# The down product of a SwiGLU layer in four parts, two of them by seven products of halves, with the results added up in DRAM

## The chip, the cores and the metric

The kernel runs on one core of one Trainium2 chip. The metric is device time in microseconds from launch to end, the median of several runs. Everything is float32; each matrix product is made of three TensorE products of rounded parts (below), so that it keeps nearly float32 accuracy.

## The reference, cut to what matters

One encoder layer on 512 tokens of width 2048. Everything up to the last line is left alone by the change; the last line is what the change is about.

```python
h2 = rms_norm(x, ffn_norm_g)                      # 512 x 2048
act = jax.nn.silu(h2 @ w_ffn_gate) * (h2 @ w_ffn_up)   # 512 x 5632
return x + act @ w_ffn_down                       # w_ffn_down: 5632 x 2048
```

## The kernel before, in words

All tensors lie transposed: 128 features in the partitions, 512 tokens along the free dimension. So `act` is 44 tiles of 128x512 (`act0` to `act43`), the output is 16 tiles of 128x512 (column tiles `m`), and a weight block is 128x128. Eight blocks make one weight tile of 128x1024, which SP loads with one DMA (`wr`).

**A plain product.** Each operand is split into a rounded part and a residual: ACT casts (`wh`, `act` first half), DVE subtracts (`wl`, `act` second half). One block times one act tile is then three matmuls of 512 columns:

```python
def mm3(ps, ah, al, bh, bl, first, last, **kw):
    mm(ps, ah, bh, first, False, **kw)
    mm(ps, ah, bl, False, False, **kw)
    mm(ps, al, bh, False, last, **kw)
```

`group()` does this for one column tile over all act tiles that are in SBUF. The split weight tiles have three buffers each, so the cast of weight tile i waits until PE has done with tile i-3.

**By seven products of halves.** The function `seven()` returns `run()`, which the gates and the FFN's gate and up products use. It takes 16 row tiles of the weights as 8 pairs, the tokens in two halves of 256, and makes two column tiles (a "group") with seven products where eight would be the plain number (the Strassen-Winograd scheme). For that, each pair of input tiles must first become seven sums of 128x256: `x_sums()` (ACT: four copies `L793` to `L797`; DVE: four sums or differences `L795` to `L800`, the last three each made from the one before) writes them to `V`, and `x_split()` splits them into `X` (ACT `L809`: one cast of 128x1792; DVE `L810`: one residual of 128x1792). Of the weights, four sums are formed on DVE (`wsum`, `L835`), and seven operands are split on ACT and DVE (`wsplit`, `L841`, `L842`). One product is

```python
for p in range(p0, p1):
    x = xs[p][:, i * 2 * H:(i + 1) * 2 * H]
    mm(bank, hi[:, p * P:(p + 1) * P], x, first and p == 0, False, skip_group_check=True)
for p in range(p0, p1):
    x = xs[p][:, i * 2 * H:(i * 2 + 1) * H]
    mm(bank[:, H:], lo[:, p * P:(p + 1) * P], x, False, p == NP - 1, skip_group_check=True)
```

that is 8 matmuls of 512 and 8 of 256 columns; all eight pairs must be there before the first product of a group can be finished. A group is 112 matmuls.

**The down product before.** `act` goes to DRAM (`actd`, by DMAs that POOL issues), but for the first four tiles. The 44 act tiles are taken in three chunks, `DOWN = (12, 16, 16)`: ACT issues the loads of a chunk (`actr`), they are split, and each of the 16 column tiles is a `group()` over the chunk, 16 x 44 x 3 = 2112 matmuls of 512 columns. The sums over chunks are kept in SBUF (`dacc`, 16 tiles); with the last chunk the residual `x2d` is loaded from DRAM, added, and SP stores `out`. Loads and short-lived tiles share five buffers, `tmp`.

**What sets the order.** Each engine runs its instructions in the order that the scheduler wrote at build time, and an instruction that waits holds up everything behind it on its engine; ACT and POOL issue their DMAs from the same queue. Matmuls keep the order of the code.

Of the kernel before, what the change touches and what calls it, by code (L numbers as in the profile page):

```python
# [41 lines left out]
DOWN = (12, 16, 16)  # L42
# [15 lines left out]
def weight_blocks():  # L58
# [20 lines left out]
    def quarters(name, c0, c1):  # L79
        for half, c in ((0, c0), (0, c1), (1, c1), (1, c0)):  # L80
            out.extend((name, k * P, c, P) for k in range(half, KT, 2))
# [10 lines left out]
    f0 = 0  # L92
    for n in DOWN:
        first = WIDE if f0 == 0 else 0
        for k in range(n if first else 0):
            out += [("w_ffn_down", (f0 + k) * P, m * P, P) for m in range(first)]
        for m in range(first, KT):
            out += cols("w_ffn_down", m * P, n, k0=f0)
        f0 += n
# [3 lines left out]
def layer_kernel(tc, wpk, xT, par, flt, zemb, w4, decT, tbl, tb2, rope, qkg, out):  # L103
# [674 lines left out]
    def seven(nm, gi):  # L778

        gain = ("ffng", "mixg")[gi]  # L780
        late, xs, raws = {}, [None] * NP, {"n": 0}
# [4 lines left out]
        def x_sums(p, xe, xo):  # L786

            V = vp.tile([P, SQ], F32, tag="V", bufs=3, name=f"{nm}V{p}")
            b12 = ev(f"b12{p}")
            v = [V[:, i * H:(i + 1) * H] for i in range(7)]  # L790
            ge, go = pcol(gain, 2 * p), pcol(gain, 2 * p + 1)
            ngo = ngain[:, gi * KT + 2 * p + 1:gi * KT + 2 * p + 2]
# [32 lines left out]
        def group_raws(n):  # L825

            t = {}
            for q, name in ((0, "a11"), (3, "a12"), (1, "a21"), (2, "a22")) if n == 0 else \
# [31 lines left out]
        def run(groups, rows, c_tiles, finish, sums=None, side_pool=None, norm=None, tail=None):  # L860
# [4 lines left out]
            banks["pool"].release()  # L865
            psf = tc.alloc_tile_pool(name="psf" + nm, bufs=1, space=PSUM, reuse_waits="tile")
            banks.update(pool=psf, n=3)

            def bank(b, n):
                return psf.tile([P, S], F32, tag=b, bufs=2 if b == "x" else 1, name=f"{nm}{b}{n}")  # L870
# [3 lines left out]

            for n in range(groups):
                w0 = group_raws(n)
# [3 lines left out]
                if n == 0:  # L880
# [51 lines left out]
                if n > 0:  # L932
                    product(z, wsplit(w0["a12"], f"a12_{n}"), 1, True)
# [3 lines left out]
                if norm and n == 0:  # L937
# [7 lines left out]
                finish(n, (c0, c1))  # L945
            state.update(tile=raws["base"] + 4 * groups, pos=BLK)
            for name in ("cp", "rc", "xb"):
                late[name].release()
            return late["sg"]
# [50 lines left out]
    def gate_finish(n, c):  # L1000
        m = n + GATES_AHEAD
        for i, t in enumerate(c):
            nc.scalar.activation(t, t, AF.Sigmoid, bias=pcol("bgate", i * KT + m))
            b = tmp(f"br{i}{m}")
            nc.scalar.dma_start(b, bd[i][m])
            nc.vector.tensor_tensor(t, t, b, ALU.mult)
        nc.vector.tensor_tensor(c[0], c[0], c[1], ALU.add)
        nc.gpsimd.dma_start(md[m], c[0])
# [24 lines left out]
    sgp = run(KT - GATES_AHEAD, [r1], c_gates, gate_finish, tail=m_first())  # L1033
# [47 lines left out]
    def act_tile(j, pool, bufs):  # L1081
        t = pool.tile([P, 2 * S], F32R, tag="act", bufs=bufs, name=f"act{j}")
        acts[j] = (t[:, :S], t[:, S:])
        return acts[j]

    def act_split(j, src, pool, bufs):
        hi, lo = act_tile(j, pool, bufs)
# [11 lines left out]
    def swiglu(n, c):  # L1099
        j, up = n // 2 * 2, n % 2  # L1100
        if not up:
            for t in c:
                nc.vector.tensor_tensor(t, t, rbc2, ALU.mult)
                nc.scalar.activation(t, t, AF.Silu)
            gated[j] = c
            return
        for i, (t, g) in enumerate(zip(c, gated.pop(j))):
            nc.vector.tensor_tensor(t, t, g, ALU.mult)
            if j + i < EARLY_ACTS:
                act_split(j + i, t, ea, EARLY_ACTS)  # L1110
            else:
                nc.gpsimd.dma_start(actd[j + i], t)

    ea = None
    sgp = run(FT, [r1, sgp], c_ffn, swiglu, sums=lambda: x_sums(NP - 1, xt[-2], xt[-1]), side_pool=early_pool,
        norm=lambda: sumsq_add(acc2, xt[-1], KT - 1, "x2sq"))
    sgp.release()
    banks["pool"].release()


    psd = tc.alloc_tile_pool(name="psd", bufs=1, space=PSUM, reuse_waits="tile")
    banks.update(pool=psd, n=8)
    r3 = tc.alloc_tile_pool(name="r3d", bufs=1, reuse_waits="tile")
    r1 = tc.alloc_tile_pool(name="r1d", bufs=1, reuse_waits="tile")
    NA = DOWN[0] - EARLY_ACTS

    def act_load(j, pool, bufs):
        t = tmp(f"actr{j}")
        nc.scalar.dma_start(t, actd[j])
        act_split(j, t, pool, bufs)  # L1130

    dacc = [None] * KT

    def down(ci, f0, n, m, dp, done=False):
        last = ci == len(DOWN) - 1
        if ci == 0:
            dacc[m] = r3.tile([P, S], F32, tag="r", bufs=16, name=f"dacc{m}")
        if last:
            x2t = tmp(f"x2r{m}")
            nc.scalar.dma_start(x2t, x2d[m])  # L1140
            nc.vector.tensor_tensor(dacc[m], dacc[m], rbc2, ALU.mult)
            nc.vector.tensor_tensor(dacc[m], dacc[m], x2t, ALU.add)
        if not done:
            group(dp, [acts[j] for j in range(f0, f0 + n)])
        if ci == 0:
            nc.scalar.copy(dacc[m], dp)
        elif not last:
            nc.vector.tensor_tensor(dacc[m], dacc[m], dp, ALU.add)
        else:
            t = tmp(f"dt{m}")  # L1150
            nc.vector.tensor_tensor(t, dp, rbc2, ALU.mult)
            nc.vector.tensor_tensor(dacc[m], dacc[m], t, ALU.add)
            nc.sync.dma_start(out[m], dacc[m])

    f0 = 0
    for ci, n in enumerate(DOWN):
        if ci == 0:
            for j in range(EARLY_ACTS, n):
                act_load(j, r1, NA)
            dps = [ps_tile(f"d0{m}") for m in range(WIDE)]  # L1160
            for k in range(n):
                for dp in dps:
                    wh, wl = wblk()
                    mm3(dp, wh, wl, acts[k][0], acts[k][1], k == 0, k == n - 1)
            for m in range(WIDE):
                down(ci, f0, n, m, dps[m], True)
        elif ci == 1:
            for p in (ea, xa, wq):
                p.release()
            r1e = tc.alloc_tile_pool(name="r1e", bufs=1, side="right", reuse_waits="tile")  # L1170
            for j in range(f0, f0 + n):
                act_load(j, r1e, 24)
        else:
            for j in range(f0, f0 + n):
# [119 lines left out]
```

## Time and profile before

| what | us |
|---|---|
| runs before: median (lowest to highest of 3) | 2619.01 (2617.99 to 2620.55) |
| the profiled execution: its own time | 2624.83 |
| the profiled execution: span from the first to the last instruction | 2623.0 |
| mean granted TensorE clock in it | 0.993 |

In the profile PE is TensorE's matmuls, PEld its weight loads, DVE VectorE, ACT ScalarE, POOL GpSimd, SP SyncE; a "q" behind a name is that engine's DMA queue. Times in rows are us from the start of the span, unless ns is said. The rows are in the section before the prediction.

### The profile page before, as it was taken

How to read it: one execution, taken by the hardware profiler on the slowest of the kernel's cores; microseconds unless marked ns; L12 is line 12 of the kernel's file. 1: busy time of each engine (PE TensorE's matmuls, PEld its weight loads, DVE VectorE, ACT ScalarE, POOL GpSimd, SP SyncE). 2: the span in 40 equal slices, each digit the busy share in tenths (PEclk: the TensorE clock that was granted, in tenths of full speed). 3: DMA queues.
4: the chain of work that ended last, by engine and by line, in shares of the span. 5: the costliest groups of instructions: out<-in, count | busy, mean ns of one | idle time of the engine just before them, and what ended most of it. 6: DMA issues, size and time to landing. Idle time of an engine off the chain costs nothing.

```text
span 2623.0 us, 33908 instructions
## 1 busy us (share of the span) xinstructions
PE 2587.8 (99%) x13170; PEld 2200.4 (84%) x13170; DVE 1811.1 (69%) x2596; ACT 1117.1 (43%) x1652; POOL 115.2 (4%) x214
## 2 busy tenths in 40 slices
PE   9999999999999999999999999999999999999999
PEld 7788888878887888788788888888888888788887
DVE  7877763756556999654799898898898862443343
ACT  6444433657344445443454444444444442421111
POOL 1000011110000000000000000000000000000000
PEclk9999999999999999999999999999999999999999
DMA  6323233222454444544233333333333342432342
GB/s 221 109 94 115 93 115 107 81 68 100 170 185 146 145 144 156 169 161 145 93 113 121 113 129 121 113 129 126 112 125 129 114 148 96 165 132 97 129 146 106
DMA packets 107469, 333.08 MB, mean 127 GB/s; under 512 B 13067, under 2 KB 14603, under 8 KB 107308
## 3 DMA queue, kind: packets, MB, share of 16 engines
q1 hardware_dynamic: 72288, 251.69, 27.7%
q10 hardware_dynamic: 22284, 40.42, 5.0%
q0 software_dynamic: 12736, 38.81, 4.2%
q8 instruction: 103, 1.69, 0.3%
q14 instruction: 58, 0.48, 0.1%
HBM read 295.21 MB, written 35.65 MB: 126 GB/s over the span
## 4 chain that ended last, share of the span: by engine, by line
PE 80%; issue 14%; DVE 2%; ACT 1%; DMA 1%; POOL 1%; SPq 0%; ACTq 0%; POOLq 0%; DVEq 0%
PE fx L121 19%; PE d L121 18%; PE fy L121 9%; PE px L121 7%; PE o L121 6%; PE fz L121 5%; PE q L121 3%; PE phv L121 3%; PE b L121 3%; PE kv L121 2%; PE g L121 1%; PE up L121 1%; PE ab L121 1%; PE kp L121 1%; PE sp L121 1%
## 5 line engine op out<-in xcount | busy, mean ns | idle before, releaser
L173 DVE TENSOR_TENSOR wl<-wr,wh 128x1024 fp32r<-128x1024 f32 (+1 forms) x242 | 289.9, 1198 | 355.8 <-ACT wh L172 354.7
L172 ACT CAST wh<-wr 128x1024 fp32r<-128x1024 f32 (+1 forms) x242 | 249.8, 1032 | 638.7 <-PE d L121 302.5
L121 PE MATMUL d<-act,wh 128*128 128x512 f32 x1408 | 436.5, 391 | 1.6 <-DVE act L1089 0.9
L121 PEld LDWEIGHTS d<-act,wh 128*128 128x128 f32 x1408 | 264.9, 188 | 59.9 <-DVE act L1089 3.3
L841 ACT CAST fwhs<-fs 128x1024 fp32r<-128x1024 f32 x176 | 185.1, 1052 | 249.7 <-PE fx L121 116.7
L121 PE MATMUL d<-act,wl 128*128 128x512 f32 x704 | 274.5, 390 | 0.0
L841 ACT CAST fwha<-fa 128x1024 fp32r<-128x1024 f32 x132 | 138.8, 1051 | 205.7 <-PE fx L121 99.6
L842 DVE TENSOR_TENSOR fwls<-fs,fwhs 128x1024 fp32r<-128x1024 f32 x176 | 214.9, 1222 | 10.8 <-ACT fwhs L841 3.6
L121 PE MATMUL fx<-fX,fwha 128*128 128x512 f32 x704 | 178.4, 395 | 3.7 <-DVE c L931 2.1
L121 PE MATMUL fx<-fX,fwhs 128*128 128x512 f32 x704 | 178.2, 395 | 1.9 <-DVE fv L857 1.9
L121 PE MATMUL fy<-fX,fwhs 128*128 128x512 f32 x704 | 177.1, 393 | 0.0
L842 DVE TENSOR_TENSOR fwla<-fa,fwha 128x1024 fp32r<-128x1024 f32 x132 | 161.2, 1221 | 5.8 <-ACT fwha L841 1.7
L121 PE MATMUL o<-ms,wh 128*128 128x512 f32 x512 | 159.9, 394 | 3.8 <-ACT wh L172 3.8
L121 PEld LDWEIGHTS d<-act,wl 128*128 128x128 f32 x704 | 132.6, 188 | 27.4
L121 PEld LDWEIGHTS fx<-fX,fwha 128*128 128x128 f32 x704 | 127.3, 190 | 27.4 <-DVE c L931 2.3
L121 PEld LDWEIGHTS fx<-fX,fwhs 128*128 128x128 f32 x704 | 127.7, 190 | 25.5 <-DVE fv L857 2.6
L121 PEld LDWEIGHTS fy<-fX,fwhs 128*128 128x128 f32 x704 | 126.8, 189 | 22.7
L121 PEld LDWEIGHTS o<-ms,wh 128*128 128x128 f32 x512 | 97.4, 191 | 24.5 <-ACT wh L172 4.3
L121 PE MATMUL px<-xh,wl 128*128 128x512 f32 x272 | 107.4, 395 | 3.0 <-DVE wl L173 3.0
L121 PE MATMUL px<-xh,wh 128*128 128x512 f32 x272 | 109.4, 402 | 0.3 <-ACT wh L172 0.2
L835 DVE TENSOR_TENSOR fs<-fa,fa 128x1024 f32<-128x1024 f32 x88 | 107.1, 1217 | 0.5 <-DMA fa<-wpk 0.2
L121 PE MATMUL px<-xl,wh 128*128 128x512 f32 x272 | 107.3, 394 | 0.0
(1134 smaller groups left out, 5195.7 us busy)
## 6 DMA issues: line engine op xcount, KB each, us to landing
wr<-wpk SPq DMA_DIRECT2D x234, 512.0 KB, 3.3
fa<-wpk SPq DMA_DIRECT2D x176, 512.0 KB, 3.5
ga<-wpk SPq DMA_DIRECT2D x52, 512.0 KB, 3.6
actd<-c POOLq DMA_DIRECT2D x40, 256.0 KB, 4.9
actr<-actd ACTq DMA_DIRECT2D x40, 256.0 KB, 3.7
bd<-bt POOLq DMA_DIRECT2D x26, 256.0 KB, 2.5
br<-bd ACTq DMA_DIRECT2D x26, 256.0 KB, 2.7
xr<-xT SPq DMA_DIRECT2D x16, 256.0 KB, 5.0
```

The costliest lines, as they stand in the source:

```text
L121: tc.keep_in_program_order(nc.tensor.matmul(out, lhsT=lhsT, rhs=rhs, start=start, stop=stop, **kw))
L172: nc.scalar.copy(st["hi"][:, c], st["raw"][:, c])
L173: nc.vector.tensor_tensor(st["lo"][:, c], st["raw"][:, c], st["hi"][:, c].bitcast(F32), ALU.subtract)
L835: nc.vector.tensor_tensor(t, a, b, ALU.add)
L841: nc.scalar.copy(hi, w)
L842: nc.vector.tensor_tensor(lo, w, hi.bitcast(F32), ALU.subtract)
```

## The change

The 44 act tiles are taken in four parts: 6 plain (`NSTD`), 16 by seven products of halves, 6 plain, 16 by halves. No part keeps its result in SBUF: each result is multiplied by the token's factor `rbc2` and added to `x2d` in DRAM by a DMA that POOL issues (`accum_op=ALU.add`); in the last part POOL copies `x2d` to `out`, DRAM to DRAM, two column tiles later, and the last two column tiles are added to a loaded `x2d` on DVE and stored by SP.

In a plain part, after every second column tile a pair of act tiles is loaded into two `tmp` buffers and made into `X` for the part by halves that follows; the result tiles `dt` take `tmp` buffers as well. The first four act tiles of a plain part lie in the pool `ea`, the other two in the pool `sg`. `seven()` is called twice more, with no gain and two `V` buffers. In `run()`, `finish` is now called for each of the two column tiles by itself, the first one ahead of the last two steps of the second; the gates and the FFN go through this too. The order of the weight blocks in DRAM follows.

```diff
-DOWN = (12, 16, 16)
+NSTD = 6
...
-    f0 = 0
-    for n in DOWN:
-        first = WIDE if f0 == 0 else 0
...
+    for f0 in (0, NSTD + KT):
+        for m in range(KT):
+            out += cols("w_ffn_down", m * P, NSTD, k0=f0)
+        for m in range(0, KT, 2):
+            quarters("w_ffn_down", m * P, (m + 1) * P, f0 + NSTD)
...
+                finish(n, 0, c0)
                 if tail and n == groups - 1:
                     tail.send(late["sg"])
                 d = ev(f"d_{n}")
                 nc.scalar.activation(d, x[:, :H], AF.Copy, scale=-1.0)
                 nc.vector.tensor_tensor(c1[:, :H], d, x[:, H:], ALU.subtract)
-                finish(n, (c0, c1))
+                finish(n, 1, c1)
...
+    def act_raw(j):
         t = tmp(f"actr{j}")
         nc.scalar.dma_start(t, actd[j])
...
+    def add_up(m, t):
+        nc.gpsimd.dma_start(x2d[m], t, accum_op=ALU.add)
...
+    def down_finish(n, i, t):
+        nc.vector.tensor_tensor(t, t, rbc2, ALU.mult)
+        add_up(2 * n + i, t)
...
+    def out_finish(n, i, t):
+        m = 2 * n + i
+        nc.vector.tensor_tensor(t, t, rbc2, ALU.mult)
+        if n < NP - 1:
+            add_up(m, t)
+            if n > 0:
+                nc.gpsimd.dma_start(out[m - 2], x2d[m - 2])
+            return
+        nc.gpsimd.dma_start(out[m - 2], x2d[m - 2])
+        nc.vector.tensor_tensor(t, t, lasts[i], ALU.add)
+        nc.sync.dma_start(out[m], t)
...
+    def last_rows(n):
+        if n == NP - 1:
+            for m in (KT - 2, KT - 1):
+                lasts.append(tmp(f"xl{m}"))
+                nc.scalar.dma_start(lasts[-1], x2d[m])
+
+    for half, f0 in enumerate((0, NSTD + KT)):
+        vp = tc.alloc_tile_pool(name=f"vpd{half}", bufs=1, reuse_waits="tile")
+        x_sums, x_split, V, run = seven("de"[half], None, 2)
+        for m in range(KT):
+            dp = ps_tile(f"d{half}{m}")
+            group(dp, [acts[j] for j in range(f0, f0 + NSTD)])
+            t = tmp(f"dt{half}{m}")
+            nc.vector.tensor_tensor(t, dp, rbc2, ALU.mult)
+            add_up(m, t)
+            if m % 2 == 0:
+                j = f0 + NSTD + m
+                V[m // 2] = x_sums(m // 2, act_raw(j), act_raw(j + 1))
+                x_split(m // 2, V[m // 2], (0, 7))
+        vp.release()
+        if half == 0:
+            run(NP, c_down, down_finish, each=early_acts, tail=act_last(NSTD + KT))
         else:
...
+            run(NP, c_down, out_finish, each=last_rows)
```

What stands on the engines at three places follows. A name carries its tile number and then a running number; the two parts by halves have names with `d` and `e` in front. In brackets is what an instruction waits for: DMASW is a DMA that POOL issued, DMAHW one that SP or ACT issued, Activation is ACT. The first place is ACT while the act tiles of the second chunk of before are loaded and split:

```order
L1088 CAST act17_20047<-actr17_20045 128x512 [waits DMAHW6_49]
L1088 CAST act18_20052<-actr18_20050 128x512 [waits DMAHW7_49]
L1129 DMA actr20_20060<-actd20_5937 128x512 [waits DVE_49]
L1088 CAST act19_20057<-actr19_20055 128x512 [waits DMAHW0_49]
L1129 DMA actr21_20065<-actd21_5938 128x512 [waits DVE_49]
L1129 DMA actr22_20070<-actd22_5939 128x512 [waits DVE_49]
L1088 CAST act20_20062<-actr20_20060 128x512 [waits DMAHW1_49]
```

The loads of later tiles stand ahead of the casts of earlier ones. ACT in the first plain part now, from the cast of pair 4 on (`wh386`, `wh387` are weight casts of the plain part):

```order
L809 CAST dX4_19529<-dV4_19519 128x7x256 [waits DVE_49,Activation_49]
L1125 DMA actr16_19588<-actd16_5933 128x512 [waits DMASW5_49,DMASW0_49]
L1125 DMA actr17_19590<-actd17_5934 128x512
L793 ACTIVATE dV5_19592<-actr16_19588 128x256 [waits DMAHW1_49]
L794 ACTIVATE db125_19593<-actr16_19588 128x256
L169 CAST wh387_19714<-wr387_19713 128x1024 [waits DMAHW7_49,PE_49]
L796 ACTIVATE dV5_19592<-actr17_19590 128x256 [waits DMAHW2_49]
L797 ACTIVATE dV5_19592<-actr17_19590 128x256
L809 CAST dX5_19602<-dV5_19592 128x7x256 [waits DVE_49,Activation_49]
L1125 DMA actr18_19655<-actd18_5935 128x512 [waits DMASW7_49,DMASW2_49]
```

Now the two loads of a pair stand behind the cast of the pair before it, and the first of them waits for a DMA of POOL's. The second place is DVE where a chunk of before begins (`dacc0` is the first column tile of the second chunk):

```order
L173 TENSOR_TENSOR wl402_20165<-wr402_20163,wh402_20164 128x1024 [waits DVE_49,PE_49,Activation_49]
L1089 TENSOR_TENSOR act27_20097<-actr27_20095,act27_20097 128x512 [waits DMAHW0_49,Activation_49]
L173 TENSOR_TENSOR wl403_20195<-wr403_20193,wh403_20194 128x1024 [waits DVE_49,PE_49,Activation_49]
L1148 TENSOR_TENSOR dacc0_19430<-dacc0_19430,d10_20100 128x512 [waits PE_49]
L1141 TENSOR_TENSOR dacc0_19430<-dacc0_19430,rbc2_11049 128x512 [waits DVE_49]
L173 TENSOR_TENSOR wl404_20227<-wr404_20225,wh404_20226 128x1024 [waits DMAHW1_49,Activation_49]
```

Residuals of weights alternate with residuals of act tiles, and the result of a column tile is added in SBUF. DVE where the first plain part ends now (`dt015` is its last column tile, `ds2` to `ds4` and `dwls2` belong to the first group by halves, `X7` to the last pair):

```order
L835 TENSOR_TENSOR ds2_0_19833<-ds1_0_19808,da11_0_19774 128x1024 [waits PE_49]
L795 TENSOR_TENSOR dV7_19732<-db127_19733,dV7_19732 128x256 [waits Activation_49]
L1186 TENSOR_TENSOR dt015_19764<-d015_19745,rbc2_11049 128x512 [waits DMAHW1_49,DMAHW5_49,DMASW0_49,PE_49]
L798 SCALAR_TENSOR_TENSOR dV7_19732<-dV7_19732,db127_19733 128x256 [waits Activation_49]
L835 TENSOR_TENSOR ds4_0_19860<-ds2_0_19833,da12_0_19780 128x1024 [waits DVE_49]
L799 SCALAR_TENSOR_TENSOR dV7_19732<-dV7_19732 128x256 [waits DVE_49]
L842 TENSOR_TENSOR dwls2_0_19836<-ds2_0_19833,dwhs2_0_19835 128x1024 [waits Activation_49]
L800 SCALAR_TENSOR_TENSOR dV7_19732<-dV7_19732 128x256 [waits DVE_49]
L835 TENSOR_TENSOR ds3_0_19884<-da11_0_19774,da21_0_19776 128x1024
L810 TENSOR_TENSOR dX7_19742<-dV7_19732,dX7_19742 128x7x256 [waits Activation_49]
```

Between the sums of pair 7 stand the last column tile's step and three steps of the coming group. The third place, ACT at the end of the second plain part, has no counterpart before (`xl14` and `xl15` are the loads of the last two column tiles of `x2d`):

```order
L797 ACTIVATE eV7_21798<-actr43_21796 128x256
L841 CAST ewhs2_0_21901<-es2_0_21899 128x1024 [waits DVE_49,PE_49]
L1177 DMA xl14_23133<-x2d14_5915 128x512 [waits DMASW6_49,DMASW5_49]
L1177 DMA xl15_23135<-x2d15_5916 128x512 [waits DMASW7_49,DMASW3_49]
L809 CAST eX7_21808<-eV7_21798 128x7x256 [waits DVE_49,Activation_49]
```

Ahead of the cast of pair 7 stand two loads that wait for DMAs of POOL's, which add the last two column tiles of the plain part to `x2d`.

## Rows read from the trace of the kernel before

**Rows 1.** The page: span, and busy time of PE and DVE.

```profile
span 2623.0 us, 33908 instructions
...
PE 2587.8 (99%) x13170; PEld 2200.4 (84%) x13170; DVE 1811.1 (69%) x2596; ACT 1117.1 (43%) x1652; POOL 115.2 (4%) x214
```

**Rows 2.** Busy time in two stretches, the FFN by halves and the plain down product.

```profile
core 0: us, PE busy (x) PEld busy (x) DVE busy (x) ACT busy (x) POOL busy (x), PEclk, DMA share, GB/s
1850.00:1900.00 50.00, 50.00 (x288) 44.06 (x287) 44.03 (x60) 22.55 (x29) 1.08 (x2) 1.00 0.33 116
2550.00:2600.00 50.00, 50.00 (x222) 41.39 (x222) 20.55 (x24) 9.49 (x9) 0.00 (x0) 1.00 0.42 147
```

**Rows 3.** The chain that ended last: start, length, engine, line.

```profile
1798.95 5.59 PE fx L121 x32
...
1818.50 5.59 PE fx L121 x32
...
2134.15 124.93 PE d L121 x551
...
2277.34 341.12 PE d L121 x1496
```

**Rows 4.** Timeline: start, duration, instruction; where down begins, and the end.

```profile
2133.03 1.12 PE L121 MATMUL fx<-fX,fwla 128*128 128x256 f32 x8
2133.98 0.63 PE L121 MATMUL d<-act,wh 128*128 128x512 f32 x2
...
2616.25 0.62 PE L121 MATMUL d<-act,wh 128*128 128x512 f32 x2
...
2616.93 0.62 PE L121 MATMUL d<-act,wh 128*128 128x512 f32 x2
...
2618.06 0.39 PE L121 MATMUL d<-act,wl 128*128 128x512 f32 x1
2618.49 0.69 DVE L1151 TENSOR_TENSOR dt<-d,rbc 128x512 f32<-128x512 f32 x1 [8.86 <-PE d L121]
...
2619.93 0.33 SPq L1153 DMA_DIRECT2D out<-dacc  x1
```

**Rows 5.** Timeline of ACT and DVE while the gates' first pair becomes X.

```profile
688.26 0.82 ACTq L972 DMA_DIRECT2D xg<-xT  x2
...
691.02 1.38 DVE L973 TENSOR_TENSOR xg<-xg,rbc 128x512 f32<-128x512 f32 x2 [0.68 <-DMA xg<-xT]
...
691.75 0.51 ACT L793 ACTIVATE gV<-xg,prm 128x256 f32<-128x256 f32 x1 [2.19 <-DVE xg L973]
...
692.96 0.49 ACT L797 ACTIVATE gV<-xg,ngain 128x256 f32<-128x256 f32 x1
...
693.49 0.43 DVE L798 SCALAR_TENSOR_TENSOR gV<-gV,gb 128x256 f32<-128x256 f32 x1 [0.37 <-ACT gV L797]
...
694.41 0.42 DVE L800 SCALAR_TENSOR_TENSOR gV<-gV 128x256 f32<-128x256 f32 x1
...
695.13 1.69 ACT L809 CAST gX<-gV 128x1792 fp32r<-128x1792 f32 x1
...
696.85 2.02 DVE L810 TENSOR_TENSOR gX<-gV,gX 128x1792 fp32r<-128x1792 f32 x1 [0.37 <-ACT gX L809]
```

**Rows 6.** DMA issues: KB each, median us from issue to landing.

```profile
actd<-c POOLq DMA_DIRECT2D x40, 256.0 KB, 4.9
actr<-actd ACTq DMA_DIRECT2D x40, 256.0 KB, 3.7
...
xg<-xT ACTq DMA_DIRECT2D x16, 256.0 KB, 2.9
```

**Rows 7.** Groups by line: count, busy us, mean ns of one, idle before.

```profile
L842 DVE TENSOR_TENSOR fwls<-fs,fwhs 128x1024 fp32r<-128x1024 f32 x176 | 214.9, 1222 | 10.8 <-ACT fwhs L841 3.6
...
L1151 DVE TENSOR_TENSOR dt<-d,rbc 128x512 f32<-128x512 f32 x16 | 11.1, 692 | 59.2 <-PE d L121 59.2
...
L172 ACT CAST wh<-wr 128x1024 fp32r<-128x1024 f32 x234 | 246.6, 1054 | 637.5 <-PE d L121 302.5 <-PE o L121 71.1 <-PE b L121 60.5
```

**Rows 8.** PE around its longest wait, and the granted clock behind it.

```profile
1095.01 0.39 PE L121 MATMUL o<-ms,wl 128*128 128x512 f32 x1
1099.24 0.74 PE L121 MATMUL o<-ms,wh 128*128 128x512 f32 x2 [3.85 <-ACT wh L172]
...
1106.90 0.39 PE L121 MATMUL o<-ms,wl 128*128 128x512 f32 x1
...
1100.00:1106.00 6.00, 5.50 (x13) 4.33 (x14) 3.05 (x4) 1.71 (x2) 0.00 (x0) 0.50 0.62 216
```

More of the change, by code (lines that the diff above doesn't have):

```diff
@@ L858, in fold, with run @@
             return t
[L860 removed]
+        def run(groups, c_tiles, finish, rows=None, sums=None, side_pool=None, norm=None, tail=None, each=None):
             raws["base"] = state["tile"]
[L865 to L867 removed]
+            if rows:
+                banks["pool"].release()
+                banks.update(pool=tc.alloc_tile_pool(name="psf" + nm, bufs=1, space=PSUM, reuse_waits="tile"), n=4)
             def bank(b, n):
[L870 removed]
+                return banks["pool"].tile([P, S], F32, tag=b, bufs=2 if b == "x" else 1, name=f"{nm}{b}{n}")
             def pool(name, **kw):
                 return tc.alloc_tile_pool(name=nm + name, bufs=1, reuse_waits="tile", **kw)
+            if not rows:
+                late["rc"] = pool("rc")
+                late["cp"] = pool("cp")
             for n in range(groups):
+                first = rows and n == 0
+                if each:
+                    each(n)
                 w0 = group_raws(n)
@@ L879, in run @@
                     next(tail)
-                if n == 0:
+                if first:
                     h11 = wsplit(w0["a11"], "a11_0")
@@ L1031, in m_first @@
         yield
-    sgp = run(KT - GATES_AHEAD, [r1], c_gates, gate_finish, tail=m_first())
+    run(KT - GATES_AHEAD, c_gates, gate_finish, rows=[r1], tail=m_first())
+    late["xb"].release()
     banks["pool"].release()
@@ L1114, in layer_kernel @@
[L1114 to L1125, printed above, removed]
@@ L1127, in act_load @@
-    def act_load(j, pool, bufs):
+        nc.vector.tensor_tensor(t, t, gated.pop(j + i), ALU.mult)
+        if j + i < EARLY_ACTS:
+            act_split(j + i, t, ea, "act", EARLY_ACTS)
+        else:
+            nc.gpsimd.dma_start(actd[j + i], t)
+    def act_raw(j):
         t = tmp(f"actr{j}")
         nc.scalar.dma_start(t, actd[j])
[L1130 to L1148, printed above, removed]
-        else:
[L1150 to L1174, printed above, removed]
-                act_load(j, r1e if j < f0 + 8 else r1, 24 if j < f0 + 8 else NA)
-        for m in range(WIDE if ci == 0 else 0, KT):
-            down(ci, f0, n, m, ps_tile(f"d{ci}{m}"))
-        f0 += n
@@ L1180, in layer_kernel, with act_last @@
-    for p in (r1e, pad, r1, r3, psd, tpool, wpool, dpool, cpool):
+        return t
+    def act_last(f0):
+        js = range(f0 + EARLY_ACTS, f0 + NSTD)
+        ts = [act_raw(j) for j in js]
+        pool = yield
+        for j, t in zip(js, ts):
+            act_split(j, t, pool, "sg", 3)
+        yield
+    ea = None
+    run(FT, c_ffn, swiglu, rows=[r1, late["sg"]], sums=lambda: x_sums(NP - 1, xt[-2], xt[-1]), side_pool=early_pool,
+        norm=lambda: sumsq_add(acc2, xt[-1], KT - 1, "x2sq"), tail=act_last(0))
@@ L1181, in layer_kernel @@
+    for p in (ea, xa, wq, pad, late["xb"], late["sg"], banks["pool"], tpool, wpool, dpool, cpool):
         p.release()
```

83 lines of the change are left out of this document (41 added, 42 removed).

## The prediction

> **What bounds the kernel now.** I read the page first: PE is busy for 2587.8 of 2623.0 us and DVE, the next, for 1811.1 [rows 1]. So TensorE is the bound, and a change is worth what it takes from PE, less the time that PE then waits. Next I read two stretches of 50 us. Both show PE busy throughout; in the FFN by halves DVE has 44.03 us, in the plain down product 20.55 [rows 2]. The reader is to see that the kernel has a stage of each kind, so the rate of both can be read here, and that DVE has less than an eighth of its time free in the kind that the change extends.
>
> By halves, the chain that ended last meets the same point of two successive groups at 1798.95 and 1818.50: 19.55 us for two column tiles of 16 act tiles [rows 3]. The plain down product begins at 2133.98 and PE's last matmul ends at 2618.06 + 0.39 = 2618.45, so it takes 484.5 us [rows 4]. Its pace is 124.93 / 551 = 0.2267 us a matmul in the chain [rows 3], as are two or three in a row at the end (2616.25 to 2616.93) [rows 4]. Nothing is waited for where it begins: the FFN's last matmuls start at 2133.03, those of down 0.95 us later [rows 4].
>
> **What PE saves.** After the change the two plain parts are 2 x 16 x 6 x 3 = 576 matmuls, 130.6 us, and the two parts by halves 16 groups of 19.55, 312.8 us. Together 443.4, against 484.5: **41.1 us less**. I take the FFN's period for these groups because one group has the same products and weight splits; a `finish` of down is one DVE multiplication per column tile, as the FFN's gate groups have.
>
> **What is late: the eight X.** A part by halves can finish no product before all eight pairs are made into X, and they are made while the plain part runs. That part is short: 288 matmuls, 65.3 us, 4.08 a column tile, 5.44 a weight tile of 24 matmuls. A pair is due every 8.16 us. What one costs is in the gates, where ACT and DVE make the same X [rows 5]: 2.76 us from the issue of the loads at 688.26 to the first instruction that uses them at 691.02; four ACT sums from 691.75 to 693.45, 1.70; three dependent DVE sums from 693.49 to 694.83, 1.34; the cast, 1.69. That makes 7.5. In the gates other pairs' loads can be ahead; here the order on ACT puts the loads of a pair behind the cast of the pair before, so these 7.5 us are one chain from pair to pair. In between stand a weight cast on ACT (1.05) or a column tile's multiplication on DVE (0.69) [rows 7]; one of them, 0.87 in the mean, gives **8.4 us a pair**, just over the 8.16 that PE allows.
>
> It starts late, too. Ahead of pair 1's ACT sums stands the cast of a weight tile that needs a buffer which PE frees after three weight tiles: 3 x 5.44 + 1.05 = 17.4. Sums, DVE and cast (1.70 + 1.34 + 1.69) bring pair 1 to 22.1, and five more pairs at 8.4 bring pair 6 to 64.1. Pair 7 has more on DVE between its sums: the multiplication of the last column tile, 0.69, and two weight operations of the coming group at 1.22 each [rows 7]; 7.5 + 3.1 = 10.6 brings its cast to 74.7. Its residual takes 2.02 [rows 5]: 76.7. PE is done with the plain part at 65.3 and has seven matmuls of the first product for pairs 0 to 6, 1.6 us: 66.9. **PE then waits 10 us, once in each half.**
>
> The landing is the weak figure. `xg`, two loads at a time, has a median of 2.9; `actr`, the loads of before from the same `actd`, as large but many in a row, 3.7 [rows 6]. Seven times the difference is 5.6, so 16 by the second. I take 12, nearer to `xg`, since two loads at a time is what happens here. The bounds: were the chain to keep PE's pace, only the end would be late. Pair 7's ACT sums would end with the plain part, then on DVE 0.69, 1.34 and 2.44 (4.5), cast 1.69 and residual 2.02, less PE's 1.6: 6.6. With the slower landing, and a further 0.4 a pair for the steps from engine to engine (0.30 from the last DVE sum to the cast [rows 5]), it is 10 + 7 x 1.3 = 19.
>
> **What the wait costs behind it.** The longest wait in the trace, 3.85 us before 1099.24, is followed by a granted clock of 0.50, the 1.2 GHz level, from 1100 to 1106 [rows 8]. There 13 matmuls take 5.50 busy us, 0.423 each against 0.2267. From 1099.24 to 1106.90 are 7.66 us, some 0.5 of it idle, so 7.16 x (1 - 0.2267 / 0.423) = **3.3 us are lost**. I count that once for each of the two waits. Could a wait three times as long cost more? The row does not tell; I leave it in the range.
>
> **The smaller terms.** In the second half ACT has, ahead of the cast of pair 7, the loads `xl14` and `xl15`, which wait for POOL's additions of the last two plain column tiles. If an addition lands as the nearest row, POOL's store `actd`, in 4.9 us [rows 6], that runs beside the DVE sums of pair 7 and adds about 1; if it takes twice that, 9.8, then 6. At the end, before, 2623.0 - 2618.45 = 4.55 us pass behind PE; now an ACT copy (0.51) and a DVE subtraction (0.42) of 128x256 stand ahead [rows 5], the multiplication and the addition are as before: +0.9.
>
> At nothing I cost `finish` in two calls in the gates and the FFN: DVE has 6 us of 50 free there [rows 2], and PE has two banks for `x`, so a DVE step that comes one step later meets a bank that PE needs a product (2.8 us, a seventh of 19.55) later. If that cover is gone it would cost up to the length of one DVE step, 0.69, in each of the FFN's 44 and the gates' 13 groups: 39. Both stages would then show a longer group; I see no step that was moved past anything PE waits for, and the sum holds nothing for it. POOL is busy 4% [rows 1], and its copies to `out` wait only for additions 20 us old.
>
> **The sum**, for the profiled execution of 2624.83: -41.1 + 2 x 12 + 2 x 3.3 + 1 + 0.9 = -8.6, so 2616.2. That execution is 5.8 above the median of 2619.0, so in the median **2610**. The change takes 41 us from PE and gives 33 back at two borders.
>
> **The rivals.** (1) The pair chain keeps PE's pace: the next pair's landing and weight casts fall into each other's gaps. Then -41.1 + 2 x 6.6 + 6.6 + 0.9 = -20.4, 2599. For it speaks that 8.4 and 8.16 are close; against, the late start of pair 1, which this chain never makes up.
>
> (2) The slower landing, 19 a border: -41.1 + 38 + 6.6 + 1 + 0.9 = +5.4, 2624. For it: `actr` is the same load, beside the same weight traffic. Against: its median comes from 16 loads in a row.
>
> (3) POOL's additions are slow, and the wait on them takes the place of PE's work: the slower side. The five `tmp` buffers are shared by result tiles and pairs, so one pair's load waits for an addition issued about 9 us (two column tiles) earlier; the order on ACT shows that wait. While an addition lands in 4.9 us, nothing waits. From some 9 on each us of landing adds one to each pair. At 9.8 that is 0.8 x 8 pairs x 2 halves = 12, and 5 more at `xl14`: -8.6 + 17 = +8, 2627. For it: no row has such a DMA, and it must read what it adds to. Against: 9.8 is twice the slowest comparable row.
>
> The Trainium skill speaks for this one: on the page "Collectives: The Full Stack", section "Part 3: Why 7× under link rate — side-by-side accounting", it says that an adding transfer reads two sources where a copy reads one, and measures about half the rate (62.28 against 32.35 GB/s, a ratio of 1.93). No run here shows it yet; as an estimate by that page, 1.93 x the store's 4.9 would be 9.5 us, just past the 9 from which it costs, and the sum about +4.
>
> **How the numbers follow.** 0.2%, 5.2 us, is about what a measurement of this kernel can tell from no change. My forecast has .50, rival 1 .17, rival 2 .15, rival 3 .18. Of the forecast, with 9 to 15 for a wait, .35 lies below 2613.8; with rival 1 that is .52 faster. The rest of the forecast, half of rival 2 and a bit of rival 3 are the same, .25; the remainder, .23, is slower. The range goes from rival 1 (2599, less 1) to rival 3 (2627, plus 3 for a longer wait at a slow clock); the forecast's own is 2604 to 2617.
>
> **What would show it.** In the profile of after: PE waits for `dX` or `eX` (`L810`) once at each part by halves, some 12 us, and the granted clock is 0.5 behind it; groups are 19.55 apart; a plain part takes 65.3; additions land in about 5; ACT's loads `actr` hardly wait for POOL's DMAs. If PE waits 6 or less at the borders, rival 1 holds; if ACT stands at `actr` for POOL's DMAs in pair after pair, rival 3. I am wrong altogether if groups of down are longer than 19.55, 16 x 0.5 us being as much as the whole forecast, or if the FFN's are.

## The result, and the profile after

The changed kernel takes 2603.94 us in the median of 7 runs (2597.75 to 2608.06), before 2617.99 (7 runs): a ratio of 0.9940, 95% interval 0.9930 to 0.9951, or 14 us less. The profiled execution took 2606.41, its span is 2604.6. The forecast was 2610, faster, in a range of 2598 to 2630; its own part of that range was 2604 to 2617, and the result lies at the lower end of it.

The page of the changed kernel, to be laid beside [rows 1]: PE is busy for 37.8 us less, and its idle time went from 35.2 to 54.6 us.

```profile
span 2604.6 us, 35152 instructions
...
PE 2550.0 (98%) x13426; PEld 2186.7 (84%) x13426; DVE 2017.0 (77%) x2902; ACT 1205.6 (46%) x1796; POOL 176.4 (7%) x290
```

PE's waits from where down begins (line, what was waited for: us in total, times, longest). All are for the `X` of a part by halves, one in the first half and two in the second:

```profile
PE ex L118 <- DVE eX L810: 13.0, 2, 10.6
PE dx L118 <- DVE dX L810: 8.6, 1, 8.6
```

PE's timeline at the points that the forecast worked with: the first plain matmul, the first product by halves with its wait, the second plain part, its border, and the last product. They answer to [rows 4].

```profile
2128.49 0.63 PE L118 MATMUL d<-act,wh 128*128 128x512 f32 x2
...
2193.80 2.08 PE L118 MATMUL dx<-dX,dwha 128*128 128x512 f32 x7
2204.50 0.79 PE L118 MATMUL dx<-dX,dwha 128*128 128x512 f32 x1 [8.62 <-DVE dX L810]
...
2224.21 2.00 PE L118 MATMUL dx<-dX,dwha 128*128 128x512 f32 x8
...
2243.76 2.00 PE L118 MATMUL dx<-dX,dwha 128*128 128x512 f32 x8
...
2257.73 2.00 PE L118 MATMUL dz<-dX,dwha 128*128 128x512 f32 x8
...
2277.28 2.00 PE L118 MATMUL dz<-dX,dwha 128*128 128x512 f32 x8
...
2361.31 0.63 PE L118 MATMUL d<-act,wh 128*128 128x512 f32 x2
...
2426.61 1.52 PE L118 MATMUL ex<-eX,ewha 128*128 128x512 f32 x6
2430.45 0.50 PE L118 MATMUL ex<-eX,ewha 128*128 128x512 f32 x1 [2.31 <-DVE eX L810]
2441.59 0.80 PE L118 MATMUL ex<-eX,ewha 128*128 128x512 f32 x1 [10.64 <-DVE eX L810]
2456.28 2.00 PE L118 MATMUL ez<-eX,ewha 128*128 128x512 f32 x8
...
2597.79 1.11 PE L118 MATMUL ex<-eX,ewla 128*128 128x256 f32 x8
```

The reader is to see here: a plain part takes 65.3 us both times (2128.49 to 2193.80, 2361.31 to 2426.61), a group 19.55 (2257.73 to 2277.28), as forecast. The first group takes 30.41 instead (2193.80 to 2224.21): 8.62 of wait and 2.24 of slow clock. At the second border the `ez` product, 13.97 behind the first product in an undisturbed group (2243.76 to 2257.73), comes at 2456.28 instead of 2440.58: 12.95 of wait and 2.75 of clock. Down ends at 2598.90 and takes 470.4 us, 14.1 less than before; the 41.1 saved were 26.6 short for the two borders and 0.4 elsewhere. Behind PE pass 5.7 us, 4.55 before.

The span fell by 18.4, more than the median. Of that, 5.5 lies ahead of down, which began at 2133.98 before and at 2128.49 after; runs 11 and 12 speak for the chance of one profiled execution.

### The profile page after: what moved, and what is told of

It reads as the page before. It is cut to its first block, busy times and chain, and to the rows that moved or that the text cites. A ratio compares the mean times of both kernels' runs of the same rounds, so it can differ in the third digit from the quotient of the medians.

```text
span 2604.6 us, 35152 instructions
## 1 busy us (share of the span) xinstructions
PE 2550.0 (98%) x13426; PEld 2186.7 (84%) x13426; DVE 2017.0 (77%) x2902; ACT 1205.6 (46%) x1796; POOL 176.4 (7%) x290
## 4 chain that ended last, share of the span: by engine, by line
PE 63%; issue 27%; DVE 4%; DMA 2%; POOL 2%; ACT 2%; SPq 0%; POOLq 0%; ACTq 0%; DVEq 0%
PE fx L118 8%; PE b L118 7%; PE px L118 7%; PE o L118 6%; PE gx L118 5%; PE fy L118 4%; PE ex L118 3%; PE q L118 3%; PE phv L118 3%; PE gy L118 3%; PE fz L118 2%; PE ey L118 2%; PE kv L118 2%; POOL x2d L1145 1%; PE g L118 1%
## 5 line engine op out<-in xcount | busy, mean ns | idle before, releaser
L170 DVE TENSOR_TENSOR wl<-wr,wh 128x1024 fp32r<-128x1024 f32 (+1 forms) x178 | 211.7, 1189 | 180.3 <-ACT wh L169 179.2
L169 ACT CAST wh<-wr 128x1024 fp32r<-128x1024 f32 (+1 forms) x178 | 182.2, 1024 | 344.5 <-PE o L118 70.3
L842 DVE TENSOR_TENSOR fwls<-fs,fwhs 128x1024 fp32r<-128x1024 f32 x176 | 214.6, 1220 | 10.6 <-ACT fwhs L841 3.8
L118 PE MATMUL d<-act,wh 128*128 128x512 f32 x384 | 118.1, 389 | 0.0
L835 DVE TENSOR_TENSOR fs<-fs,fa 128x1024 f32<-128x1024 f32 x88 | 107.0, 1215 | 0.1
L118 PEld LDWEIGHTS fx<-fX,fwla 128*128 128x128 f32 x704 | 96.5, 191 | 7.0
L118 PEld LDWEIGHTS fy<-fX,fwls 128*128 128x128 f32 x704 | 96.2, 190 | 6.9
```

What stands on the lines that cost most here:

```text
L118: tc.keep_in_program_order(nc.tensor.matmul(out, lhsT=lhsT, rhs=rhs, start=start, stop=stop, **kw))
L169: nc.scalar.copy(st["hi"][:, c], st["raw"][:, c])
L170: nc.vector.tensor_tensor(st["lo"][:, c], st["raw"][:, c], st["hi"][:, c].bitcast(F32), ALU.subtract)
L835: nc.vector.tensor_tensor(t, a, b, ALU.add)
L842: nc.vector.tensor_tensor(lo, w, hi.bitcast(F32), ALU.subtract)
```

## The experiments

All ran beside the kernel before on the same chip; ratios are to it, with 95% intervals, from five rounds each. Waits are PE's waits for `dX` and `eX` in the profile, 8.6 and 13.0 in the changed kernel. Differences to the changed kernel are differences of medians. By the width of the intervals two kernels are told apart from some 4 us on (0.0016 in the ratio), and smaller differences may be chance. Each wait comes from one profiled execution. How far chance moves it can be seen where an edit leaves the pairs of a half alone: the first wait was 8.6 in the changed kernel, 7.4 in run 1 and 11.3 in run 11. So a wait that moves by less than 4 us is no evidence by itself.

**1. The loads of the last two column tiles issued by POOL.**

```diff
-                nc.scalar.dma_start(lasts[-1], x2d[m])
+                nc.gpsimd.dma_start(lasts[-1], x2d[m])
```

> The loads xl14 and xl15 are issued by POOL instead of ACT. Theory (the wait of PE at a border is the lateness of the last cast): in the changed kernel the last DVE sum of pair 7 ended at 2435.74 and its cast began at 2437.79, so the cast comes 2 us earlier, the wait at the second border falls from 13.0 (2.3 + 10.6) to about 11, and the time by 2 us to about 2602. Rival (these loads make all the difference between the two borders, 13.0 against 8.6): 4.4 us, to about 2599.5.

2601.0 us, 0.9934 (0.9920 to 0.9948), not told apart from the changed kernel; waits 7.4 and 11.0 (2.6 + 8.4). The second fell by the forecast 2, but that is within chance. The step itself is plain in the traces: in this run the last DVE sum of pair 7 ended at 2435.24 and the cast began at 2435.32, 0.08 later instead of 2.05. This is ACT in the changed kernel at that place (timeline): pair 7's last DVE sum ended at 2435.74, ACT's queue stood in the two loads from 2432.52 on.

```profile
2432.52 5.18 ACTq L1177 DMA_DIRECT2D xl<-x2d  x2
2437.79 1.69 ACT L809 CAST eX<-eV 128x1792 fp32r<-128x1792 f32 x1 [5.13 <-DMA x2d<-dt]
```

The bracket says 5.13, but ACT would have waited for the sums most of that time anyway. So these loads cost 2.05 there and not the whole difference of 4.4 between the borders; in the second half the first pair also waited 3.3 for an addition.

**2. Pairs earlier.**

```diff
-            if m % 2 == 0:
-                j = f0 + NSTD + m
+            if m in (0, 1, 2, 4, 6, 8, 10, 12):
+                p = (0, 1, 2, 4, 6, 8, 10, 12).index(m)
+                j = f0 + NSTD + 2 * p
...
```

> Pairs are made after column tiles 0, 1, 2, 4, 6, 8, 10, 12 instead of 0, 2, ..., 14. Theory (the pairs are one chain of about 8.5 us each that starts too late): the last X is some 8 us earlier in each half, the waits fall from 8.6 and 13.0 to about 1 and 5, and with part of the clock loss behind them the time falls by 16 to 19, to about 2586. Rival 1 (the weight work of the coming group on ACT and DVE at the border sets the wait, whenever the pairs are made): only the stretch of pair 7's chain goes, 3 us a border, 6 in all, to about 2598. Rival 2 (pairs asked for sooner crowd out weight casts, and PE waits inside the plain part): the same time as the changed kernel, 2604, with PE waits for wh or wl in the plain part.

2590.3 us, 0.9891 (0.9877 to 0.9904), 13.6 below the changed kernel and, with run 8, the fastest of all. PE's waits for `X` in it:

```profile
PE ex L118 <- DVE eX L810: 3.0, 1, 3.0
PE dx L118 <- DVE dX L810: 1.6, 1, 1.6
```

So the borders' loss can be had back, and neither rival holds. But two things changed at once: the order on ACT shows that most pairs' loads now stand ahead of the cast of the pair before. Runs 5, 6 and 7 take that apart.

**3. Stored, not added.**

```diff
-        nc.gpsimd.dma_start(x2d[m], t, accum_op=ALU.add)
+        nc.gpsimd.dma_start(x2d[m], t)
```

> The DMAs that add results to x2d store them without adding, so the sum over the four parts and x2 is left out. Theory (additions land soon enough, 5.2 and 5.7 us, and almost nothing waits for them): waits at the borders as in the changed kernel within 1 us, landing some 4.9, time 2604 less 0 to 3. Rival (the reading addition holds the tmp buffers and so delays pair after pair): the waits fall by 5 or more each, time 2594 or less.

2598.8 us, 0.9923 (0.9910 to 0.9935), 5 below the changed kernel, which is hardly more than chance; waits 7.2 and 7.4. This is between the two: the second wait fell by more than chance, so the additions do cost something there. In the DMA view (KB each, median us from issue to landing), first the changed kernel:

```profile
actr<-actd ACTq DMA_DIRECT2D x40, 256.0 KB, 4.5
x2d<-dt POOLq DMA_DIRECT2D x32, 256.0 KB, 5.2
x2d<-dc POOLq DMA_DIRECT2D x30, 256.0 KB, 5.7
```

and without the addition:

```profile
actr<-actd ACTq DMA_DIRECT2D x40, 256.0 KB, 3.8
x2d<-dt POOLq DMA_DIRECT2D x32, 256.0 KB, 2.8
x2d<-dc POOLq DMA_DIRECT2D x30, 256.0 KB, 4.4
```

An addition lands 2.4 us later than a store in the plain parts, a ratio of 1.86, and 1.3 later by halves. The gain sits at the second border, where the cast of pair 7 came 70.7 us after the part's first matmul instead of 76.5. Only some 2.7 of these 5.8 lie where ACT waits for additions by name, ahead of the first pair (1.3 up to pair 1's cast) and ahead of the last cast (1.4). The rest, 3.2, was gained from pair 1 to pair 6, where the casts were 8.0 us apart in the mean instead of 8.7; there the pairs' own loads landed in 3.5 instead of 4.7 (medians of that plain part). In both halves (8.2 a pair in the first) the chain then kept about PE's pace of 8.16, and waits of 7.2 and 7.4 were left all the same.

The Trainium skill, page "Collectives: The Full Stack", section "Part 3: Why 7× under link rate — side-by-side accounting", has an adding transfer at about half the rate of a copy (1.93, measured on collectives of four ranks). The ratio of landing times in the plain parts, 1.86, is of that size; by halves, where the store alone takes 4.4, it is 1.3.

**4. Pairs one column tile later.**

```diff
-            if m % 2 == 0:
-                j = f0 + NSTD + m
+            if m in (1, 3, 5, 7, 9, 11, 13, 15):
+                p = (1, 3, 5, 7, 9, 11, 13, 15).index(m)
+                j = f0 + NSTD + 2 * p
...
```

> Pairs are made after column tiles 1, 3, ..., 15, one column tile (4.08 us) later each. Theory (chain of pairs): each wait grows by about 4, to 12.5 and 17, time +8, about 2612. Rival 1 (the work of the coming group at the border sets the wait): no change within 2 us, 2604.

2609.7 us, 0.9960 (0.9947 to 0.9972), 5.7 above the changed kernel; waits 14.5 (5.9 + 8.6) and 12.1 (4.1 + 8.0). The first grew by 6, the second, within chance, not at all. Later pairs cost time, but the wait does not follow the place one to one.

**5. Pairs from 1 on one column tile earlier.**

```diff
-            if m % 2 == 0:
-                j = f0 + NSTD + m
+            if m in (0, 1, 3, 5, 7, 9, 11, 13):
+                p = (m + 1) // 2
+                j = f0 + NSTD + 2 * p
...
```

> Half a step: pair 0 after column tile 0, pairs 1 to 7 after column tiles 1, 3, ..., 13, that is one column tile (4.08 us) earlier than in the changed kernel; buffers as in the changed kernel. Theory (the wait follows the place of the pairs one to one): waits of 8.6 and 13.0 fall to about 4.5 and 9, time -8 and some of the clock, about 2595. Rival (half of the early pairs' gain came from loads that moved ahead of casts, which here happens only at every second pair): waits fall by 2 or less each, 2600 or more.

2606.6 us, 0.9951 (0.9940 to 0.9963): not faster, waits 13.5 and 10.6. That is a miss for the theory as put; the rival's time came, but not its waits, since the first one grew. The trace shows why. ACT, pairs 3 to 7 of the first half (casts, the issue of loads, the first sum):

```profile
2165.67 1.71 ACT L809 CAST dX<-dV 128x1792 fp32r<-128x1792 f32 x1 [1.06 <-DVE dV L800]
2165.77 0.86 ACTq L1125 DMA_DIRECT2D actr<-actd  x2
2171.44 0.42 ACT L793 ACTIVATE dV<-actr 128x256 f32<-128x256 f32 x1 [4.07 <-DMA actr<-actd]
...
2174.54 0.87 ACTq L1125 DMA_DIRECT2D actr<-actd  x2
2176.18 1.70 ACT L809 CAST dX<-dV 128x1792 fp32r<-128x1792 f32 x1 [2.45 <-DVE dV L800]
...
2184.30 1.70 ACT L809 CAST dX<-dV 128x1792 fp32r<-128x1792 f32 x1 [1.06 <-DVE dV L800]
2184.38 0.88 ACTq L1125 DMA_DIRECT2D actr<-actd  x2
2191.14 0.42 ACT L793 ACTIVATE dV<-actr 128x256 f32<-128x256 f32 x1 [5.13 <-DMA actr<-actd]
...
2194.04 0.81 ACTq L1125 DMA_DIRECT2D actr<-actd  x2
2198.53 1.68 ACT L809 CAST dX<-dV 128x1792 fp32r<-128x1792 f32 x1 [5.11 <-DVE dV L800]
...
2205.43 1.69 ACT L809 CAST dX<-dV 128x1792 fp32r<-128x1792 f32 x1 [3.04 <-DVE dV L800]
```

The order puts the loads of pairs 3, 5 and 7 ahead of a cast, those of 4 and 6 behind one. From cast to cast it takes 10.5 to pair 4, 8.1 to pair 5, 14.2 to pair 6, 6.9 to pair 7; in the second half the same alternation, 10.2, 8.0, 12.7, 6.9 from casts at 36.6, 46.8, 54.8, 67.5 and 74.4 behind the part's first matmul. (The 14.2 also holds DVE's weight work for the coming group, with ACT waiting 5.1 for the sums.) A load behind the cast costs ACT's first sum a wait of 4 to 5 us here (in the first half of the changed kernel the pairs from 2 on wait 1.0 to 2.9). So the link is real; which pairs have it is decided by the scheduler's order, not by the column tile alone.

**6. Loads in buffers of their own, ahead of the sums of the pair before.** Same column tiles; `V` gives up one of its two buffers.

```diff
-        x_sums, x_split, V, run = seven("de"[half], None, 2)
+        x_sums, x_split, V, run = seven("de"[half], None, 1)
+
+        def pair_load(p):
+            ts = []
+            for j in (f0 + NSTD + 2 * p, f0 + NSTD + 2 * p + 1):
+                ts.append(vp.tile([P, S], F32, tag="pr", bufs=4, name=f"pr{j}"))
+                nc.scalar.dma_start(ts[-1], actd[j])
+            return ts
+
+        raw = {0: pair_load(0)}
...
-                V[m // 2] = x_sums(m // 2, act_raw(j), act_raw(j + 1))
...
+                if p + 1 < NP:
+                    raw[p + 1] = pair_load(p + 1)
+                V[p] = x_sums(p, *raw[p])
...
```

> The pairs' loads have four buffers of their own (V keeps one buffer instead of two, for the space) and each pair's loads are issued ahead of the sums of the pair before; pairs are made after the same column tiles as in the changed kernel. Theory (the load that stands behind the cast of the pair before is the link that stretches the chain): from pair 2 on the casts come at PE's pace and pair 7's comes 3 to 5 us earlier than at 72.2 and 76.5 after the part's first matmul; waits about 4 and 8, time 8 to 10 below the changed kernel, about 2595. Rival (the place of the pair among the column tiles sets the chain, since ACT's weight casts, which wait for PE, stand between the pairs): casts and waits stay as they were within 1.5 us, time 2601 to 2604, and the gain of the early pairs came from their place.

2599.6 us, 0.9927 (0.9914 to 0.9940), not told apart from the changed kernel. PE's waits for `X`:

```profile
PE ex L118 <- DVE eX L810: 14.4, 2, 10.0
...
PE dx L118 <- DVE dX L810: 0.9, 1, 0.9
```

The two halves come apart. In the first, with no pair moved, the wait fell from 8.6 to 0.9: pair 7's cast came at 64.2 behind the part's first matmul instead of 72.2 (70.6 in run 1, 74.8 in run 11). That refutes the rival there. In the second it rose to 14.4. ACT there, pairs 4 to 6:

```profile
2396.97 1.05 ACT L169 CAST wh<-wr 128x1024 fp32r<-128x1024 f32 x1 [3.22 <-DMA wr<-wpk]
...
2404.28 0.42 ACT L794 ACTIVATE eb<-pr 128x256 f32<-128x256 f32 x1 [5.33 <-DMA pr<-actd]
...
2423.21 1.68 ACT L809 CAST eX<-eV 128x1792 fp32r<-128x1792 f32 x1 [5.27 <-DVE eV L800]
```

A weight tile that landed late (3.2), a load (5.3) and DVE's part of pair 6 (5.3) each held the chain, and ahead of the first pair ACT waited 4.5 for an addition. With one `V` buffer a pair's first sum also waits for the residual of the pair before, 5.7 in five waits of this half; but it is 7.3 in five waits of the first, so this alone does not set the halves apart. What does was not separated.

**7. Loads issued by SP.**

```diff
-    def act_raw(j):
+    def act_raw(j, pair=False):
         t = tmp(f"actr{j}")
-        nc.scalar.dma_start(t, actd[j])
+        (nc.sync if pair else nc.scalar).dma_start(t, actd[j])
...
-                V[m // 2] = x_sums(m // 2, act_raw(j), act_raw(j + 1))
+                V[m // 2] = x_sums(m // 2, act_raw(j, True), act_raw(j + 1, True))
```

> The loads of the pairs are issued by SP, so they no longer stand behind the cast of the pair before on ACT; the pairs are made after the same column tiles as in the changed kernel. Theory (the load behind the cast is a link of the chain): without about 3 us of it a pair takes 5 to 6, so the chain follows PE's 8.16 and only the end is late; waits fall from 8.6 and 13.0 to about 4 and 7, time about 2592 to 2595. Rival 1 (DVE and ACT at the border set the wait, the loads do not matter): no change, 2604. Rival 2 (SP's weight loads now stand behind loads that wait for tmp buffers): PE waits for weights inside the plain part, 2604 or more.

2606.8 us, 0.9957 (0.9945 to 0.9970); waits 11.5 and 12.3. No gain, and the theory's number is missed. SP issued pair 2's loads 22.2 us after the part's first matmul; on ACT, behind pair 1's cast, they had gone at 20.6. So the loads came no earlier for the other queue. Both of the suspects held them: ahead of them on SP's queue two weight loads waited 6.2 and 1.7 us for DVE, and then the loads themselves 3.1 for an addition.

**8. Early pairs and POOL's `xl` loads together** (edits 1 and 2).

> The pairs after column tiles 0, 1, 2, 4, ..., 12, and xl14 and xl15 issued by POOL: both edits together. Theory (both act on the same chain): the wait of 3.0 that was left at the second border falls to about 1, the one at the first stays at 1.6; time 2 us below the 2590.3 of the early pairs alone, about 2588. Rival (with the pairs early, cast and loads no longer stand in one another's way): no change, 2590.

2591.3 us, 0.9895 (0.9879 to 0.9910), waits 2.2 and 3.6. The rival: with the pairs early, the loads stand behind the cast of pair 7 (in run 2 it began at 2418.58, the first load was issued at 2423.52).

**9. Own buffers, early pairs, POOL's loads** (edits 1, 2 and 6).

> The buffers of the run before, with the pairs after column tiles 0, 1, 2, 4, ..., 12 and xl14 and xl15 issued by POOL. Theory (loads and place each act on one chain): the last X is there when PE asks for it, waits for dX and eX under 1 us each; against the early pairs with shared buffers (2590, waits of 1.6 and 3.0) 4 us less, about 2586. Rival (what is left is the weight work of the coming group on DVE): waits of 1 to 3 stay, 2590.

2596.6 us, 0.9918 (0.9905 to 0.9931); waits 1.6 and 11.9. Worse than the early pairs alone, and again only in the second half, so the theory that the two add up is wrong with these buffers.

**10. A pair after each of the first eight column tiles** (the list in edit 2 is 0 to 7).

> A pair after each of the first eight column tiles (0 to 7), buffers and loads as in the changed kernel. With the pairs after 0, 1, 2, 4, ..., 12 the casts came 5.9 to 9.9 us apart and the waits were 1.6 and 3.0. Theory (the chain runs at its own pace when nothing of the plain part's order stands in it): pair 7's cast comes by 60 after the part's first matmul, no wait at either border, time 5 below the early pairs' 2590, about 2585. Rival (pairs and weights then share the DMA engines and ACT in the first half of the part): PE waits for wh or wl inside the plain part, 2590 or more.

2603.3 us, 0.9948 (0.9934 to 0.9961). PE's longest wait, by its total:

```profile
PE d L118 <- DVE wl L170: 14.6, 7, 4.2
```

No wait for `X` is left (the other two waits, 1.8 and 1.6, are for other steps of DVE), and 14.6 us of waits for weights have come up inside the plain parts: the rival. The stall moved, it did not go.

**11 and 12. `finish`, joined again in the changed kernel, and split in the kernel before with nothing else changed.** The diff is the first one's; the second makes the change's own edits of `run()` and of the gates' and the FFN's `finish` in the kernel before.

```diff
-                finish(n, 0, c0)
                 if tail and n == groups - 1:
...
+                finish(n, 0, c0)
                 finish(n, 1, c1)
```

> In the changed kernel finish is called for both column tiles after the last product, as before the change. In the trace of before, the product by w_br before the FFN (matmuls o) took 181.5 us from its first to its last matmul start and the FFN 872.0; after the change 178.2 and 870.7. Theory A (the split finish moves the loads and casts at the border of the gates): joined, o takes some 181 again and the FFN 872, down begins 4 us later and the time is about 2608. Theory B (the difference is chance of one profiled execution): o stays within 1 us of 178.5, time 2604.

> The kernel before with nothing changed but finish, called for each column tile by itself in the gates and the FFN. Theory A: o takes some 178.5 instead of 181.5, the FFN 870.7 instead of 872, time 4 us below before, ratio 0.9985. Theory B (chance): no change against before, o at 181 or scattered.

Joined: 2605.9 us, 0.9950 (0.9937 to 0.9964), within the scatter of the changed kernel's runs. Split alone: 2617.6, 0.9993 (0.9984 to 1.0001). The product `o` (tile view: count, ns lowest/median/highest, first to last start) before, joined, and split alone:

```profile
L121 PE MATMUL o<-ms,wh x512: 389/389/628, 1078.9 to 1260.4; 128*128 128x512 f32 x171
```

```profile
L118 PE MATMUL o<-ms,wh x512: 387/389/628, 1076.7 to 1255.4; 128*128 128x512 f32 x171
```

```profile
L121 PE MATMUL o<-ms,wh x512: 389/389/632, 1073.2 to 1251.7; 128*128 128x512 f32 x171
```

181.5, 178.7 and 178.5: theory B. The joined kernel has the short `o` without the split, so some 3 of the 5.5 us ahead of down in the trace pair were that execution's long wait for a weight tile [rows 8]. Down begins at 2127.2 in the joined kernel and between 2122.6 and 2130.9 in the traces with the split, so chance alone moves it by more than the rest. By the ratios the split alone brings no gain that can be told from nothing; up to 4 us would lie within the interval.

## Why the prediction was right

**What PE saves: right.** 65.3 a plain part and 19.55 a group stand in the timeline, the group to the hundredth.

**The chain of pairs: right in its end, by two errors that cancel.** Forecast were casts that end at 22.1 (pair 1), 64.1 (pair 6) and 74.7 (pair 7) after the part's first matmul, and PE at work again at 76.7. Measured: 22.0, 64.8, 73.9 and 76.0. The late start was there: the weight cast ahead of pair 1's sums began 16.33 us after the part's first matmul, where 3 x 5.44 = 16.32 were forecast. The 8.4 us a pair in between (8.6 measured from pair 1 to 6) were made of other parts, as from pair 4 to pair 5 (timeline of ACT):

```profile
2173.08 1.70 ACT L809 CAST dX<-dV 128x1792 fp32r<-128x1792 f32 x1
2173.16 0.81 ACTq L1125 DMA_DIRECT2D actr<-actd  x2
2177.65 0.42 ACT L793 ACTIVATE dV<-actr 128x256 f32<-128x256 f32 x1 [2.87 <-DMA actr<-actd]
...
2181.91 1.70 ACT L809 CAST dX<-dV 128x1792 fp32r<-128x1792 f32 x1 [1.98 <-DVE dV L800]
```

The loads stand behind the cast in the order, but they are issued 0.08 us after it begins, not after it ends (within 0.9 of its begin for every pair of this half). So the cast's 1.69 runs beside the landing and is no term of the chain, as the forecast had it. Against that the loads took 4.49 from issue to first use (3.4 to 4.8 for pairs 2 to 6) instead of 2.76. The one error is 1.7 too much, the other about as much too little, and that they cancel is luck. The four sums took 1.33 instead of 1.70, and up to pair 4 ACT's weight casts waited for PE. ACT in the first half of the changed kernel (waits: total, times, longest):

```profile
ACT wh L169 <- PE d L118: 11.0, 5, 4.2
ACT dV L793 <- DMA actr<-actd: 10.1, 6, 2.9
```

**The wait: mis-sized a little.** 12 a border were taken, by a choice between 10 and 16; the working itself had given 10. Measured are 8.6 and 12.95. The step that failed is that choice: the slower landing was added on top of a chain that counted the cast as well. From the working's 10 to the 8.6 it is the same error once more: from the cast of pair 6 to that of pair 7 passed 9.1 us, not 10.6; the load, which took 2.64 there, ran beside the cast of pair 6. For the second half the number of 12 + 1 is met, but by other terms: the last cast came 4.3 later than in the first half, 2.05 of it at `xl14` and `xl15`, which the sum held at 1, the rest on the way to pair 6, where it held nothing, and the chain was cheaper than the 12.

**The clock behind the wait: a third too large.** 2.24 and 2.75 instead of 3.3. The granted clock fell to the level of [rows 8], and the longer wait did not cost more, the question that was left open (windows: PE busy, PEclk, DMA share, GB/s; first the row of before at the end of its wait, then the first border, then the second):

```profile
1099.00:1100.00 1.00, 0.74 (x2) 0.92 0.22 20
```

```profile
2202.00:2204.50 2.50, 0.00 (x0) 0.50 1.06 315
2204.50:2207.00 2.50, 2.50 (x10) 0.50 1.00 350
2207.00:2209.00 2.00, 2.00 (x9) 0.86 0.99 382
```

```profile
2439.00:2441.50 2.50, 0.00 (x0) 0.50 1.03 403
```

At the two borders the clock is at 0.50 while PE still waits, in [rows 8] it fell only once PE was at work again (0.92 in the microsecond in which the wait ends, 0.50 from 1100 on). So a part of the slow stretch passed in the long waits, where it costs nothing.

**Nothing for `finish`: not contradicted** by runs 11 and 12. **The tail: right**, 1.1 for 0.9.

**The rivals.** The result lies between the forecast and rival 1 (the chain keeps PE's pace), which had 6.6 a border and 2599: the first border's 8.6 is nearer to it than to 12, the second's 12.95 is not. Where the chain did keep that pace, in run 3, 7.2 and 7.4 were left. Rival 2 had the landing right (4.5 even exceeds its 3.7) and the time wrong, since the cast beside the landing gave it back. Rival 3 did not come: additions land in 5.2 to 5.7, short of the 9 from which they would hold each pair. What they cost is about 5 us (run 3, hardly clear of chance), of which the sum held 1; and about half of it came in a way that no rival had, by making the pairs' own loads land later.

Summed, the forecast for down was 9.5 us less and 14.1 came: 3.4 of the difference is the first border's wait, 1.6 the clock, and 0.4 goes the other way. What stays open is why one order on ACT puts a pair's loads behind a cast and another does not (it follows from the scheduler, run 5), and what held the second half in runs 6 and 9.

## What to carry to other kernels

When operands of a next stage are prepared under the stage before, work out the chain of one of them and the place where the first can start; a chain that is only as fast as the cover shows its late start in full at the border (run 3: about 8.1 a pair, and 7 of wait). Look at where a load stands in the queue of its issuing engine: behind the last step of the item before, its landing becomes a link (4 to 5 us in run 5), but counted from the start of that step, which runs beside it. Asking earlier pays until the preparation collides with the cover's own operands: with pairs after 0, 1, 2, 4, ... it took 2590, with pairs after 0 to 7 2603, and there the stall had only changed its place.

## What was not expected

A plain part keeps the DMA engines busy at 0.84 for 213 GB/s, against 0.42 for 147 before [rows 2]: twice the share for less than half more bytes (windows of the changed kernel; PE, PEld, DVE, ACT, POOL busy, PEclk, DMA share, GB/s):

```profile
2130.00:2195.00 65.00, 65.00 (x289) 53.77 (x287) 49.80 (x65) 32.92 (x49) 13.56 (x16) 1.00 0.84 213
```

The same stretch of run 3, where results are stored and not added, has 0.68 for 222 GB/s:

```profile
2132.00:2195.00 63.00, 63.00 (x280) 52.16 (x279) 49.64 (x65) 32.52 (x48) 8.71 (x17) 1.00 0.68 222
```

By these rows the additions take some of the engines' time for no more bytes. With them a load of 256 KB takes 4.5 us to land, without them 3.8 (run 3), where the same size took 2.9 to 3.7 in [rows 6]. And DVE, at 49.8 of 65, is nearly as full there as by halves (33.0 of 40 from 2550 to 2590), so a plain part gives far less cover than it gave before.
